# Normalizing the sparse attention's queries in row form, ahead of their split

## The chip, the cores and the metric

The kernel runs on one core of a Trainium2 chip. The metric is the device time of one execution in microseconds (us). TensorE is called PE (its weight loads PEld), VectorE DVE, ScalarE ACT, GpSimd POOL, and the queue that issues most loads SP.

## The reference

A decoder block over 512 tokens of width 2048: RMSNorm, one projection, eight heads of sparse attention (NSA) and four of gated linear attention, an output projection, cross attention over 256 memory tokens, and a SwiGLU. What matters here is how an NSA head treats its queries (cut):

```python
def rms_norm(u, g):
    y = u * lax.rsqrt(jnp.mean(u * u, axis=-1, keepdims=True) + EPS)
    return y * g
qn = rms_norm(q, g_q) * (NSA_DK ** -0.5)          # per head, 128 wide
s = einsum(qn, kc) - slope * (t - cmp_mid);  p = softmax(where(vis, s, NEG))
...
s = einsum(qn, kw) - slope * (t - pos);      p = softmax(...)
```

Each head has three branches: compressed blocks (31 keys, held as 32 columns), selected blocks (512 tokens are 8 blocks of 64, and up to 16 are chosen, so all are taken) and a causal window. The 8 heads share 2 sets of keys and values.

## The kernel before

Every large product runs as three fp32r products of high and low parts (`mm3`: hi·hi, hi·lo, lo·hi, so 2 + 1 matmuls of 128x512 per tile). `split` makes the parts: a copy to fp32r on ACT (hi) and a subtraction on DVE (lo). Weights come by SP into a buffer `w` (2 of them), and are split into `wh` and `wl` (3 each).

The projection of the block's input is walked tile by tile. `in_tile(16 + n)` is one tile of 128 columns: 48 matmuls into a bank `mm`, with 8 calls of `flows.tick()` in it. The heads are Python generators (`nsa_head`, `head_norm`), run in the ticks: `yield n` lets n ticks pass. So a head's steps are written out between the matmuls of the projection of later tiles, and what the generators emit in a tick sets the order on each engine; a scheduler with priorities moves it a little. A tick has 6 matmuls of 128x512 behind it. PSUM has 3 banks `mm`, 2 `s`, 2 `t` and one `o`.

The life of a head: its projected tile (features on partitions, tokens in columns) is split into `Q` hi and lo; the squares (`n`) are summed over the partitions for each token; after W_SUM ticks the sums are used, after W_NORM more the head waits until the head before it has taken its scores (`("s", h - 1)`), and then takes one score block per 2 ticks in a bank `s` (first branch on `KS`, 416 and 512 wide with the 32 compressed columns ahead, second on `KV`), with a bias made by ACT from the distances, a reduction on DVE to the minimum (the scores are negated), and an Exp on ACT. When its head before has left `o`, the P matrices are transposed (PE, into `t`), split into `PH` and `PL` and multiplied with the values into `o`. The end is a normalization of `o` (squares `on`, `column_sums` with `ones_r`).

The head before does not normalize its queries. It keeps them raw but for the gain, and carries one factor per token through the softmax: `sc` (inverse root mean square times the token's own `rc`), `neg = -sc` and `sl = slope / sc`, each of shape 128 x 4 (tile `qs`). To have them with tokens on partitions, it sums the squares by four fp32 matmuls, each with 128 tokens of `n` as weights and the vector `one` (a column of `vecs`) as the moving side, into a bank `s`.

The first head starts ahead of the value weights' stage (`natural(w_vsw, ...)`, with the compression weights `w_c`); heads 1 to 7 are interleaved with the swish gates of the other attention in the order `IN_ORDER`; then the last two gates (`w_r67`) are projected together in two banks, with a tick per 6 matmuls, and `flows.drain()` runs what is left of the heads. The output projection `w_out` follows; its first two tiles (16 products each over the mixed heads, `X`) are filled in between the last heads' steps, and the 16th product needs head 7.

Of the kernel before, what the change touches and what calls it, by code (L numbers as in the profile page):

```python
# [39 lines left out]
IN_ORDER = (1, 2, 8, 3, 9, 4, 10, 5, 11, 6, 12, 7, 13)  # L40
TOFF = (0, 512, 896, 1152)

W_SUM, W_NORM, W_LEVEL = 3, 2, 2

LAG = 3

# [14 lines left out]
def hybrid_block(ctx: ExitStack, tc: tile.TileContext, x_t, mem_t, sv, cmat, umask, w_a, w_r67, w_v, w_vg, w_v3,  # L61
# [17 lines left out]
    def small(tag, bufs):  # L79
        return sb([128, 32], tag, bufs)  # L80
# [7 lines left out]
    def bank(tag):  # L88
        return psp.tile([128, 512], F32, name=tag, tag=tag, bufs={"mm": 3, "s": 2, "t": 2, "o": 1}[tag])
# [3 lines left out]
    def row(tag, dt=F32):  # L93
        return sb([128, 512], tag, BUFS[tag], dt)
# [61 lines left out]
    def split(hi, lo, src, gain=None):  # L156

        if gain is None:
            return S.copy(hi, src), V.tensor_sub(lo, src, hi)  # L159
        return (S.activation(hi, src, AF.Copy, scale=gain),  # L160
                V.scalar_tensor_tensor(lo, src, gain, hi, op0=OP.mult, op1=OP.subtract))
# [85 lines left out]
    def column_sums(sq, cols=T, tag="n", ps="s", wait=1, ahead=0):  # L247

        hi, lo = row(tag, F32R)[:, :cols], row(tag, F32R)[:, :cols]
        with tc.high_priority(offset=ahead):  # L250
            split(hi, lo, sq)
        yield wait
        ps = bank(ps)[:, :cols]
        mm(ps, ones_r, hi, start=True, stop=False)
        mm(ps, ones_r, lo, start=False, stop=True)
        return ps
# [14 lines left out]
        inv_rms(rc, ps[:, :tiles], n, const.tile([128, 32], F32, name="rt", tag="rt", bufs=1)[:, :tiles])  # L271
        return rc

    def head_norm(ps, rs, gain, dst, cols=T):
        q1 = row("q1")[:, :cols]
        if len(rs.shape) == 3:
            V.tensor_mul(q1.rearrange("p (a n) -> p a n", a=2), ps.rearrange("p (a n) -> p a n", a=2), rs)
        else:
            V.tensor_mul(q1, ps, rs)
        sq = row("n")[:, :cols]  # L280
        S.activation(sq, q1, AF.Square)
        pn = yield from column_sums(sq, cols, wait=W_SUM)
        r, t = row("n")[:, :cols], row("n")[:, :cols]
        inv_rms(r, pn, 128, t)
        if isinstance(dst, tuple):
            V.scalar_tensor_tensor(t, q1, gain, r, op0=OP.mult, op1=OP.mult)
            split(*dst, t)
        else:
            V.scalar_tensor_tensor(dst, q1, gain, r, op0=OP.mult, op1=OP.mult)
# [89 lines left out]
    nc.sync.dma_start(cm, cmat[:, 128:768])  # L379
    flows.until(lambda: "col" in norm)  # L380
    rs, rc = norm["row"], norm["col"]
    rc2 = small("rc2", 1)[:, :NT]
    V.tensor_mul(rc2, rc, rc)
    vl = [natural_end(acc, 0, 512, rc, lambda i: row("KV"))]
    um = [row("M").bitcast(U32) for _ in range(2)]
    gkr, gk2, ga = row("st")[:96], row("M", F32R)[:96], row("M", F32R)[:96]
# [330 lines left out]
    def nsa_head(h, ps):  # L717
        kv = h // 4
        slope = 2.0 ** -(h + 1)
        qn = row("Q", F32R), row("Q", F32R)  # L720
        split(*qn, ps, g_q)
        sq = row("n")
        S.activation(sq, ps, AF.Square)
        yield W_SUM
        pn = bank("s")
        for i in range(NT):
            mm(pn[:, i:i + 1], sq[:, 128 * i:128 * i + 128], one, start=True, stop=True)
        qs = triple("qs")
        sc, sl, neg = qs[:, 0], qs[:, 1], qs[:, 2]
        V.tensor_mul(neg, pn[:, :NT], rc2)  # L730
        inv_rms(sc, neg, 128, sl)
        V.tensor_mul(sc, sc, rc)
        V.reciprocal(sl, sc)
        V.tensor_scalar(sl, sl, slope, None, op0=OP.mult)
        V.tensor_scalar(neg, sc, -1.0, None, op0=OP.mult)
        yield W_NORM
        while not {"kc", ("k", 0, kv), ("k", 1, kv)} <= done or h and ("s", h - 1) not in done:
            yield 1
        sm = triple("sm")
        mn = triple("mn")  # L740
        cf = triple("cf")

        def coefficients(b):
            V.reciprocal(cf[:, b, :], sm[:, b, :])
            V.tensor_mul(cf[:, b, :], cf[:, b, :], gates[:, :, 3 * h + b])

        pc, pc3 = sb([128, NT, 32], "pc", 1), sb([128, NT, 3, 32], "pc3", 1)

        def visible(i, s):
            V.scalar_tensor_tensor(pc[:, i], cdist[:, 32 * i:32 * i + 32], sl[:, i:i + 1], s, op0=OP.mult, op1=OP.add)  # L750

        def weigh_blocks():
            V.tensor_reduce(mn[:, 0, :], pc, axis=AX.X, op=OP.min)
            V.tensor_sub(pc, mn[:, 0, :][:, :, None].to_broadcast([128, NT, 32]), pc)
            V.tensor_mul(pc, pc, sc[:, :, None].to_broadcast([128, NT, 32]))
            S.activation(pc, pc, AF.Exp)
            V.reduce_sum(sm[:, 0, :], pc, axis=AX.X)
            coefficients(0)
            V.tensor_mul(pc3, pc[:, :, None, :].to_broadcast([128, NT, 3, 32]),
                         cf[:, 0, :][:, :, None, None].to_broadcast([128, NT, 3, 32]))  # L760

        ps_ = []

        def scale(b):
            coefficients(1 + b)
            for i in range(NT):
                n = 128 * (i + 1)
                pi = ps_[b][:, POFF[i]:POFF[i] + n]
                V.tensor_scalar(pi, pi, cf[:, 1 + b, i:i + 1], None, op0=OP.mult)

        for b in range(2):
            p = sb([128, 1280], "P", 2)
            ps_.append(p)
            for i in range(NT):
                n = 128 * (i + 1)
                pi = p[:, POFF[i]:POFF[i] + n]
                S.activation(pi, dist[:, 512 - n:], AF.Copy, scale=sl[:, i:i + 1])
                s = bank("s")
                q = part(qn, 128 * i, 128)
                c = 32 if b == 0 and i < 3 else 0  # L780
                mm3(s[:, :c + n], q, part(keys[b][kv], 0 if b or c else 32, c + n), start=True, stop=True)
                if c and i == 0:
                    mm3(s[:, 160:192], part(qn, 384, 128), part(keys[0][kv], 0, 32), start=True, stop=True)
                    visible(3, s[:, 160:192])
                if c:
                    visible(i, s[:, :32])
                s = s[:, c:c + n]
                m = mn[:, 1 + b, i:i + 1]
                V.tensor_tensor_reduce(pi, s, pi, scale=1.0, scalar=3e38, op0=OP.add, op1=OP.min, accum_out=m)
                V.tensor_mul(m, m, sc[:, i:i + 1])  # L790
                S.activation(pi, pi, AF.Exp, bias=m, scale=neg[:, i:i + 1], accum_out=sm[:, 1 + b, i:i + 1])
                yield 2 if h < NH - 1 else 1
            if b == 0:
                weigh_blocks()
            scale(b)
        done.add(("s", h))

        while "vc" not in done or h and ("a", h - 1) not in done:
            yield 1
        pct = bank("t")  # L800
        for i in range(NT):
            PE.transpose(pct[:96, 128 * i:128 * i + 128], pc3[:, i].rearrange("p r n -> p (r n)"), ident)
        pcs = row("e", F32R)[:96]
        S.copy(pcs, pct[:96])
        V.tensor_sub(pcs[64:], pct[64:96], pcs[64:])
        o = None
        for b in range(2):
            pt = sb([128, 1280], "PH", PTB, F32R), sb([128, 1280], "PL", PTB, F32R)

            def turn(j):  # L810
                n = 128 * (NT - j)
                tp = bank("t")
                for i in range(j, NT):
                    PE.transpose(tp[:, 128 * (i - j):128 * (i - j) + 128],  # L814
                                 ps_[b][:, POFF[i] + 128 * j:POFF[i] + 128 * j + 128], ident)
                split(*part(pt, TOFF[j], n), tp[:, :n])

            def weigh(j):
                n = 128 * (NT - j)
                mm3(o[:, 128 * j:], part(vsw[j], 256 * b + 128 * kv, 128), part(pt, TOFF[j], n),  # L820
                    start=False, stop=b == 1 and j == NT - 1)

            turn(0)
            yield 2
            if b == 0:
                o = bank("o")
                mm(o, vc[:, 128 * kv:128 * kv + 128], pcs, start=True, stop=False)
            for j in range(1, NT):
                turn(j)
                weigh(j - 1)  # L830
                yield 2
            weigh(NT - 1)
        done.add(("a", h))
        t = row("st" if h < 4 else "M")
        S.copy(t, o)
        sq = row("on")
        S.activation(sq, t, AF.Square)
        pn = yield from column_sums(sq, T, "on", "t", W_SUM)
        r = row("on")
        inv_rms(r, pn, 128, row("on"))  # L840
        V.scalar_tensor_tensor(t, t, vec("g_nsa"), r, op0=OP.mult, op1=OP.mult)
        mix[h] = spill(t) if h < 4 else t
# [963 lines left out]
```

## Time and profile before

| what | value |
|---|---|
| median of 3 runs | 2296.41 us (2295.43 to 2296.8) |
| profiled execution | 2296.01 us, its span 2294.1 us |
| granted clock | 0.999 |
| PE busy | 2282.2 us, 99% of the span |
| PEld, DVE, ACT, POOL busy | 83%, 72%, 52%, 7% |
| chain that ended last | PE 92%, DMA 3%, DVE 3%, ACT 1%, issue 1% |

Reading it: "busy" is the time in which at least one instruction ran on the engine; a busy PE may still issue with gaps between its matmuls. The span is measured on the engines, the time of the execution from outside, 1.9 us more. A line number is that of the code above. In a group "out<-in" stands for the names of the tiles, and "x8" for eight records.

### The profile page before, as it was taken

What the parts mean: (1) busy time and instruction counts of PE and PEld (TensorE: products, weight loads), DVE (VectorE), ACT (ScalarE), POOL (GpSimd) and SP (SyncE); (2) the same over time, 40 slices, a digit from 0 to 9 for tenths busy, and PEclk for the clock granted to TensorE, in tenths of its full rate; (3) what the DMA queues carried; (4) which work ended last, traced back from release to release, by engine and by line L of the source; (5) the groups of instructions that cost most, each with busy time, mean ns of one, the idle gap of its engine ahead of it and who ended that gap; (6) DMA issues with size and microseconds to landing.
All of it is one profiled execution on the core that took longest, in us unless ns stands there. A gap on an engine that the chain in (4) does not pass through costs nothing.

```text
span 2294.1 us, 29540 instructions
## 1 busy us (share of the span) xinstructions
PE 2282.2 (99%) x10773; PEld 1896.1 (83%) x10773; DVE 1663.2 (72%) x2555; ACT 1182.6 (52%) x1855; POOL 163.7 (7%) x240
## 2 busy tenths in 40 slices
PE   9999999999999999999999999999999999999999
PEld 7988888888888888787888888888888888888887
DVE  6478866677775446688788788888887875775685
ACT  6334545566774345665545445554554565444452
POOL 0011100011110000110000000000000000000000
PEclk9999999999999999999999999999999999999999
DMA  6577656466655334685556656565665598766754
GB/s 197 136 192 180 172 157 168 127 173 174 164 170 170 133 134 138 217 233 174 168 182 208 186 162 200 184 191 158 205 201 164 165 326 298 264 233 249 263 209 147
DMA packets 140593, 434.17 MB, mean 189 GB/s; under 512 B 14464, under 2 KB 35200, under 8 KB 136992
## 3 DMA queue, kind: packets, MB, share of 16 engines
q1 hardware_dynamic: 80752, 306.83, 39.8%
q0 software_dynamic: 33824, 96.75, 17.6%
q10 hardware_dynamic: 25872, 28.71, 3.5%
q8 instruction: 84, 1.38, 0.2%
q14 instruction: 61, 0.50, 0.1%
HBM read 390.81 MB, written 94.11 MB: 211 GB/s over the span
## 4 chain that ended last, share of the span: by engine, by line
PE 92%; DMA 3%; DVE 3%; ACT 1%; issue 1%; SPq 0%; DVEq 0%; ACTq 0%
PE mm L99 49%; PE t L99 17%; PE s L99 14%; PE o L99 9%; DVE wl L159 1%; PE t L814 1%; PE s L1377 1%; DMA w<-w_c 1%; DMA raw<-w_down 0%; DMA st<-x_t 0%; DMA w<-w_vsw 0%; ACT wh L159 0%; DMA raw<-w_gu 0%; PE t L1599 0%; DMA w<-w_v 0%
## 5 line engine op out<-in xcount | busy, mean ns | idle before, releaser
L159 ACT CAST qh<-raw 128x1024 fp32r<-128x1024 f32 (+1 forms) x526 | 510.4, 980 | 491.9 <-PE t L99 126.5
L159 DVE TENSOR_TENSOR ql<-raw,qh 128x1024 fp32r<-128x1024 f32 (+1 forms) x526 | 591.4, 1133 | 150.0 <-PE mm L99 52.7
L99 PE MATMUL mm<-X,wh 128*128 128x512 f32 x1600 | 504.5, 395 | 0.0
L99 PEld LDWEIGHTS mm<-X,wh 128*128 128x128 f32 x1600 | 294.3, 188 | 56.2 <-issue 0.8
L99 PE MATMUL t<-qh,PB 128*128 128x512 f32 x968 | 335.9, 392 | 0.0
L99 PE MATMUL mm<-X,wl 128*128 128x512 f32 x800 | 314.0, 393 | 0.1
L99 PE MATMUL mm<-qh,PB 128*128 128x512 f32 x868 | 311.1, 391 | 2.3 <-ACT qh L159 2.0
L159 DVE TENSOR_TENSOR wl<-w,wh 128x1024 fp32r<-128x1024 f32 (+2 forms) x150 | 179.6, 1200 | 157.3 <-ACT wh L159 155.5
L159 ACT CAST wh<-w 128x1024 fp32r<-128x1024 f32 (+2 forms) x150 | 154.2, 1029 | 242.0 <-PE mm L99 171.7
L99 PE MATMUL s<-qh,PB 128*128 128x512 f32 x672 | 232.7, 391 | 0.0
L99 PE MATMUL mm<-qh,PA 128*128 128x512 f32 x640 | 221.8, 390 | 0.0
L99 PEld LDWEIGHTS t<-qh,PB 128*128 128x128 f32 x968 | 182.0, 188 | 37.1
L99 PEld LDWEIGHTS mm<-qh,PB 128*128 128x128 f32 x868 | 163.2, 188 | 37.8 <-ACT qh L159 3.7
L99 PE MATMUL t<-ql,PB 128*128 128x512 f32 x484 | 188.6, 390 | 0.0
L99 PE MATMUL o<-qh,PB 128*128 128x512 f32 x484 | 188.0, 390 | 0.0
L99 PEld LDWEIGHTS mm<-X,wl 128*128 128x128 f32 x800 | 150.3, 188 | 32.4 <-DVE wl L159 1.5
L99 PE MATMUL mm<-ql,PB 128*128 128x512 f32 x434 | 169.9, 391 | 0.1
L99 PEld LDWEIGHTS s<-qh,PB 128*128 128x128 f32 x672 | 126.2, 188 | 25.7 <-ACT qh L159 0.2
L99 PEld LDWEIGHTS mm<-qh,PA 128*128 128x128 f32 x640 | 120.2, 188 | 25.1
L99 PE MATMUL s<-ql,PB 128*128 128x512 f32 x336 | 131.5, 391 | 0.1
L99 PE MATMUL mm<-ql,PA 128*128 128x512 f32 x320 | 124.7, 390 | 0.0
L1279 DVE TENSOR_TENSOR raw<-raw 128x1024 f32<-128x1024 f32 x80 | 97.8, 1223 | 31.4 <-DMA raw<-w_gu 31.4
(501 smaller groups left out, 3452.5 us busy)
## 6 DMA issues: line engine op xcount, KB each, us to landing
raw<-w_gu SPq DMA_DIRECT2D x88, 768.0 KB, 4.4
raw<-w_gu SPq DMA_DIRECT2D x88, 512.0 KB, 3.6
raw<-w_down SPq DMA_DIRECT2D x84, 512.0 KB, 4.7
td<-w_down POOLq DMA_DIRECT2D x66, 512.0 KB, 6.5
w<-w_a SPq DMA_DIRECT2D x60, 512.0 KB, 4.2
raw<-td SPq DMA_DIRECT2D x22, 1024.0 KB, 4.8
PB<-h POOLq DMA_DIRECT2D x35, 512.0 KB, 5.4
h<-T ACTq DMA_DIRECT2D x66, 256.0 KB, 3.9
```

What stands on the lines that cost most here:

```text
L99: last_mm[0] = PE.matmul(*args, **kw)
L159: return S.copy(hi, src), V.tensor_sub(lo, src, hi)
L814: PE.transpose(tp[:, 128 * (i - j):128 * (i - j) + 128], ps_[b][:, POFF[i] + 128 * j:POFF[i] + 128 * j + 128], ident)
L1279: V.tensor_sub(raw[:, 0:1024], raw[:, 0:1024], raw[:, 512:1536])
L1377: PE.transpose(ps[f][:, 128 * i:128 * i + 128], hs[i][:, c:c + 128], ident)
```

## The change

The projected queries go through `head_norm`, as the keys do: times `rs` (the tokens' factor in row form) into `q1`, squares, sums over the partitions by `column_sums` (a split of the squares, two fp32r matmuls of 128x512 with `ones_r`), an inverse root on full rows 128x512, one multiplication by gain and root, and only then the split into `Q`. The factors `sc`, `neg`, `sl` and the products with them are gone; bias and Exp have constants as scale. The bank for the sums is `s` for head 0, `mm` for the others. The wait W_NORM behind the normalization goes from 2 ticks to 7.

```diff
-W_SUM, W_NORM, W_LEVEL = 3, 2, 2
+W_SUM, W_NORM, W_LEVEL = 3, 7, 2
...
-    def head_norm(ps, rs, gain, dst, cols=T):
+    def head_norm(ps, rs, gain, dst, cols=T, sums="s"):
...
-        pn = yield from column_sums(sq, cols, wait=W_SUM)
+        pn = yield from column_sums(sq, cols, ps=sums, wait=W_SUM)
...
-    rc2 = small("rc2", 1)[:, :NT]
-    V.tensor_mul(rc2, rc, rc)
...
         qn = row("Q", F32R), row("Q", F32R)
-        split(*qn, ps, g_q)
-        sq = row("n")
-        S.activation(sq, ps, AF.Square)
-        yield W_SUM
-        pn = bank("s")
-        for i in range(NT):
-            mm(pn[:, i:i + 1], sq[:, 128 * i:128 * i + 128], one, start=True, stop=True)
-        qs = triple("qs")
-        sc, sl, neg = qs[:, 0], qs[:, 1], qs[:, 2]
-        V.tensor_mul(neg, pn[:, :NT], rc2)
-        inv_rms(sc, neg, 128, sl)
-        V.tensor_mul(sc, sc, rc)
-        V.reciprocal(sl, sc)
-        V.tensor_scalar(sl, sl, slope, None, op0=OP.mult)
-        V.tensor_scalar(neg, sc, -1.0, None, op0=OP.mult)
+        yield from head_norm(ps, rs, g_q, qn, sums="mm" if h else "s")
         yield W_NORM
...
-            V.scalar_tensor_tensor(pc[:, i], cdist[:, 32 * i:32 * i + 32], sl[:, i:i + 1], s, op0=OP.mult, op1=OP.add)
+            V.scalar_tensor_tensor(pc[:, i], cdist[:, 32 * i:32 * i + 32], slope, s, op0=OP.mult, op1=OP.add)
...
-            V.tensor_mul(pc, pc, sc[:, :, None].to_broadcast([128, NT, 32]))
...
-                S.activation(pi, dist[:, 512 - n:], AF.Copy, scale=sl[:, i:i + 1])
+                S.activation(pi, dist[:, 512 - n:], AF.Copy, scale=slope)
...
-                V.tensor_mul(m, m, sc[:, i:i + 1])
-                S.activation(pi, pi, AF.Exp, bias=m, scale=neg[:, i:i + 1], accum_out=sm[:, 1 + b, i:i + 1])
+                S.activation(pi, pi, AF.Exp, bias=m, scale=-1.0, accum_out=sm[:, 1 + b, i:i + 1])
```

Line numbers of the changed kernel are 2 lower up to the head, and 18 lower behind it (the reduction L789 is L772, the Exp L791 is L773, the bias L777 is L760, the scaling L769 is L752, the swish lines L857 to L862 are L839 to L844).

In the places below X is an input or a mixed head in two parts, wh and wl are weights. First PE in a head in the middle of the stretch, before: `n` are the squares, `vecs` holds the vector of ones.

```order
L99 MATMUL mm<-X,wh 128x512 x2
L99 MATMUL mm<-X,wl 128x512
L99 MATMUL s<-KS,Q 128x416 x3
L99 MATMUL s<-KS,Q 128x512 x3
L99 MATMUL mm<-X,wh 128x512 x2
L99 MATMUL s<-vecs,n 128x1 x4
L99 MATMUL mm<-X,wl 128x512
L99 MATMUL mm<-X,wh 128x512 x2
L99 MATMUL mm<-X,wl 128x512
L99 MATMUL mm<-X,wh 128x512 x2
```

The same head's sums now:

```order
L99 MATMUL s<-KS,Q 128x160 x3
L99 MATMUL s<-KS,Q 128x32 x3
L99 MATMUL mm<-X,wh 128x512 x2
L99 MATMUL mm<-X,wl 128x512
L99 MATMUL mm<-X,wh 128x512 x2
L99 MATMUL mm<-X,wl 128x512
L99 MATMUL mm<-n,ones_r 128x512 x2
L99 MATMUL mm<-X,wh 128x512 x2
L99 MATMUL mm<-X,wl 128x512
L99 MATMUL mm<-X,wh 128x512 x2
L99 MATMUL mm<-X,wl 128x512
```

Four fp32 matmuls of one column gave way to two of 512 columns in a bank `mm`, and the score blocks of the head before stand elsewhere between the projection's matmuls.

Second, PE at the end of the heads, before: `mm<-X,wh` up to the transposes of P are the last gates' projection, `s<-KS,Q` and `s<-KV,Q` the scores of head 7.

```order
L99 MATMUL mm<-X,wh 128x512 x2
L99 MATMUL mm<-X,wl 128x512
L99 MATMUL s<-KS,Q 128x416 x3
L99 MATMUL s<-KS,Q 128x512 x3
L99 MATMUL mm<-X,wh 128x512 x2
L99 MATMUL s<-KV,Q 128x128 x3
L99 MATMUL mm<-X,wl 128x512
L99 MATMUL mm<-X,wh 128x512 x2
L99 MATMUL s<-KV,Q 128x256 x3
L99 MATMUL mm<-X,wl 128x512
L99 MATMUL mm<-X,wh 128x512 x2
L99 MATMUL mm<-X,wl 128x512
L814 MATMUL t<-ident,P 128x128 x4
```

And now, where the rows of `mm` behind the transposes belong to the output projection:

```order
L99 MATMUL mm<-X,wh 128x512 x2
L99 MATMUL mm<-X,wl 128x512
L99 MATMUL mm<-X,wh 128x512
L99 MATMUL o<-PH,KV 128x128
L99 MATMUL mm<-X,wh 128x512
L99 MATMUL s<-KS,Q 128x416 x3
L99 MATMUL s<-KS,Q 128x512 x3
L99 MATMUL o<-PL,KV 128x128
L99 MATMUL s<-KV,Q 128x128 x3
L99 MATMUL s<-KV,Q 128x256 x3
L99 MATMUL o<-PH,KV 128x128
L796 MATMUL t<-ident,P 128x128 x3
```

Head 7's scores stood among the matmuls of the gates' projection; now they stand behind its last one, with products of head 6's P around them.

Third, ACT at the same place, before (`L858` to `L860` is the swish, `L777` the bias, `L791` the Exp):

```order
L159 CAST PH<-t 128x384
L159 CAST X<-KS 128x512
L159 CAST wh<-w 128x1024
L858 ACTIVATE st<-q_6306 128x512
L777 ACTIVATE P<-cm,qs 128x128
L777 ACTIVATE P<-cm,qs 128x256
L777 ACTIVATE P<-cm,qs 128x384
L777 ACTIVATE P<-cm,qs 128x512
L859 ACTIVATE st<-st,vecs 128x512
L791 ACTIVATE P,sm<-P,mn,qs 128x128
L791 ACTIVATE P,sm<-P,mn,qs 128x256
L860 ACTIVATE st<-st 128x512
```

And now (swish L840 to L842, bias L760, Exp L773):

```order
L773 ACTIVATE P,sm<-P,mn 128x256
L841 ACTIVATE st<-st,vecs 128x512
L773 ACTIVATE P,sm<-P,mn 128x384
L842 ACTIVATE st<-st 128x512
L773 ACTIVATE P,sm<-P,mn 128x512
L739 ACTIVATE pc<-pc 128x128
L840 ACTIVATE st<-q_6216 128x512
L159 CAST PH<-t 128x512
L841 ACTIVATE st<-st,vecs 128x512
L159 CAST PH<-t 128x384
L842 ACTIVATE st<-st 128x512
L159 CAST X<-M 128x512
```

Between head 7's bias and the cast of the next operand of the output projection (`X<-M`) stand now the four Exps of a branch, both gates' swish and two casts of head 6's P; before, several casts of X stood ahead of the bias.

Fourth, DVE in the stage of the value weights, before, around head 0's normalization:

```order
L161 SCALAR_TENSOR_TENSOR Q<-mm,vecs,Q 128x512
L159 TENSOR_TENSOR Q<-e,Q 128x4x64 x2
L613 TENSOR_TENSOR e<-KV,vecs 128x8x31 x2
L730 TENSOR_TENSOR qs<-s,rc_539 128x4
L243 SCALAR_TENSOR_TENSOR qs<-qs 128x4
L244 TENSOR_SCALAR qs<-qs 128x4
L245 TENSOR_TENSOR qs<-qs 128x4
L732 TENSOR_TENSOR qs<-qs,rc 128x4
L733 RECIPROCAL qs<-qs 128x4
L735 TENSOR_SCALAR qs<-qs 128x4
L734 TENSOR_SCALAR qs<-qs 128x4
L159 TENSOR_TENSOR wl<-w,wh 128x1024
```

And now:

```order
L159 TENSOR_TENSOR wl<-w,wh 128x1024
L279 TENSOR_TENSOR q_3197<-mm,rs 128x512
L159 TENSOR_TENSOR wl<-w,wh 128x1024
L159 TENSOR_TENSOR n<-n 128x512
L243 SCALAR_TENSOR_TENSOR n<-s,n 128x512
L244 TENSOR_SCALAR n<-n 128x512
L159 TENSOR_TENSOR wl<-w,wh 128x1024
L245 TENSOR_TENSOR n<-n 128x512
L286 SCALAR_TENSOR_TENSOR n<-q_3197,vecs,n 128x512
L159 TENSOR_TENSOR Q<-n,Q 128x512
L159 TENSOR_TENSOR wl<-w,wh 128x1024 x2
L734 SCALAR_TENSOR_TENSOR pc<-cm,s 128x32 x2
```

The split of Q (L161) and eight small operations on 128x4 gave way to seven operations on 128x512, spread between the splits of weights, and head 0's first block (`pc<-cm,s`) comes two splits of weights further behind.

## The prediction

> **What bounds the kernel now.** I read the page's first and fourth parts, then the stretch of the heads by windows, then the waits and the order of time in two windows. The lines of the engines and of the chain:
>
> ```profile
> PE 2282.2 (99%) x10773; PEld 1896.1 (83%) x10773; DVE 1663.2 (72%) x2555; ACT 1182.6 (52%) x1855; POOL 163.7 (7%) x240
> PE 92%; DMA 3%; DVE 3%; ACT 1%; issue 1%; SPq 0%; DVEq 0%; ACTq 0%
> ```
>
> PE is the bound, and the chain lies on it. So only matmuls taken away and stalls of PE count. The stretch with the heads falls in three windows (columns: stretch, its length, busy us and instructions of PE, PEld, DVE, ACT, POOL, then the granted clock, DMA share and rate):
>
> ```profile
> 345.00:405.00 60.00, 58.66 (x297) 48.72 (x296) 37.21 (x88) 32.76 (x59) 4.45 (x6) 1.00 0.62 168
> 405.00:640.00 235.00, 235.00 (x1237) 198.06 (x1238) 167.30 (x489) 150.40 (x330) 36.31 (x49) 1.00 0.59 156
> 640.00:692.00 52.00, 51.89 (x256) 41.21 (x255) 41.89 (x98) 37.60 (x78) 5.89 (x11) 1.00 0.61 197
> ```
>
> In the middle, heads 1 to 7 beside the projection, PE is never idle, and DVE and ACT are free for 29% and 36% of it. In the first window, the value weights, PE idles 1.3 us; in the last, the end of the heads, 0.1. The clock is full in all three.
>
> **The sums on PE.** One group of sums before, and two fp32r matmuls with `ones_r` in the end of a head, as the change uses them (start, length, what):
>
> ```profile
> 423.56 0.95 PE L99 MATMUL s<-vecs,n 128*128 128x1 f32 x8
> 424.38 0.71 PE L99 MATMUL mm<-X,wh 128*128 128x512 f32 x2
> 424.93 0.39 PE L99 MATMUL mm<-X,wl 128*128 128x512 f32 x1
> ...
> 499.98 0.61 PE L99 MATMUL t<-on,ones_r 128*128 128x512 f32 x2
> 500.43 0.62 PE L99 MATMUL mm<-X,wh 128*128 128x512 f32 x2
> ```
>
> From the start of the sums to the `wl` matmul at 424.93 are 1.37 us. Two matmuls of 512 columns are 0.45 (499.98 to 500.43), so the pair at 424.38 accounts for 0.45 of this and the sums for 0.92. The new sums take 0.45. That is 0.47 less per head, 3.8 us for eight, straight on the path. It can't be much more (nothing of the group is left); it is nothing if the gaps were filled by something else, which I see nowhere.
>
> Here a rule speaks against the change. The Trainium skill, "TensorE: Matmul & The Clock Gate" (Step-by-step: what each phase is for), says "throughput is purely `N cycles`": one column a cycle; "FP8 and Floating Point Precision" (TensorE Precision Notes) gives true fp32 four passes. By that four fp32 matmuls of one column are 16 cycles, next to nothing, and two of 512 are 1024: the change would add 0.45 us per head instead of saving 0.47. The rows say otherwise for the old group, 0.92 us; for the new one rule and row agree.
>
> **DVE and ACT, per head.** Rows of the middle window (mean ns is the last number before the bar):
>
> ```profile
> L790 DVE TENSOR_TENSOR mn<-mn,qs 128x1 f32<-128x1 f32 x48 | 7.5, 157 | 1.1
> L161 DVE SCALAR_TENSOR_TENSOR Q<-mm,vecs,Q 128x512 fp32r<-128x512 f32 x7 | 5.2, 747 | 0.0
> L857 DVE TENSOR_TENSOR q<-mm,rs 128x512 f32<-128x512 f32 x6 | 4.1, 692 | 7.0 <-PE mm L99 7.0
> L243 DVE SCALAR_TENSOR_TENSOR on<-t,on 128x512 f32<-128x512 f32 x5 | 3.5, 691 | 0.4
> L841 DVE SCALAR_TENSOR_TENSOR st<-st,vecs,on 128x512 f32<-128x512 f32 x4 | 3.0, 752 | 0.1
> L244 DVE TENSOR_SCALAR on<-on 128x512 f32<-128x512 f32 x5 | 2.1, 426 | 0.1
> L755 DVE TENSOR_TENSOR pc<-pc,qs 128x128 f32<-128x128 f32 x6 | 1.7, 290 | 0.0
> L730 DVE TENSOR_TENSOR qs<-s,rc 128x4 f32<-128x4 f32 x7 | 1.1, 162 | 5.8 <-PE s L99 5.7
> ...
> L160 ACT ACTIVATE Q<-mm,vecs 128x512 fp32r<-128x512 f32 x7 | 4.8, 681 | 0.0
> L240 ACT ACTIVATE on<-t,vecs 128x512 f32<-128x512 f32 x6 | 4.1, 683 | 0.0
> L242 ACT ACTIVATE on<-on 128x512 f32<-128x512 f32 x6 | 3.8, 640 | 0.0
> L241 ACT ACTIVATE on<-on 128x512 f32<-128x512 f32 x6 | 3.8, 626 | 0.0
> L159 ACT CAST on<-on 128x512 fp32r<-128x512 f32 x6 | 3.7, 610 | 0.0
> L240 ACT ACTIVATE qs<-qs,vecs 128x4 f32<-128x4 f32 x7 | 2.0, 286 | 4.8 <-DVE qs L730 4.8
> ```
>
> DVE loses the split's low part (0.75), eight small operations (0.16 each by L730, 1.3), one of 128x128 (0.29) and eight of 128x1 (1.26): 3.6 us. It gains the product with `rs` (0.69 as L857), two low parts and the last product of the root (0.69 each, as L243), L243, L244 (0.43) and the gain (0.75 as L841): 4.6. ACT loses the gain (0.68) and three small ones (0.29 or less each, 0.8) and gains three of 128x512 (0.68, 0.63, 0.64) and two casts (0.61 each): 1.7 more. In the middle, with 34 us per head (7 groups of sums, L730, in 235 us) and DVE and ACT with 10 and 12 free of it, both are hidden behind PE; if the cover went, it would cost 1.0 and 1.7 us a head. The factors `rc2`, once, are as small as L730. No DMA of this kernel is added or taken away; the orders to POOL that hang on ticks move with them.
>
> **The banks.** Sums in `mm` need one of three banks, for the 3 ticks at most that one DVE and one ACT read take; the projection's result leaves its bank with the first product. PE is never late here before, so I take nothing; a missed bank would be a stall of under 1 us (one product, 0.69) per head.
>
> **The first stage, 345 to 405.** PE waits here for the splits of the weights, and the splits stand in DVE's queue with head 0's softmax:
>
> ```profile
> 389.30 0.74 PE L99 MATMUL mm<-wh,X 128*128 128x512 f32 x2 [0.79 <-ACT wh L159]
> 390.56 0.50 PE L99 MATMUL mm<-wl,X 128*128 128x512 f32 x1 [0.28 <-DVE wl L159]
> ...
> 378.63 0.69 DVE L789 CUSTOM_DVE_ANT_0 P<-s,P 128x512 f32<-128x512 f32 x1
> 381.12 1.28 DVE L769 TENSOR_SCALAR P<-P,cf 128x128 f32<-128x128 f32 x4
> 382.31 2.35 DVE L159 TENSOR_TENSOR wl<-w,wh 128x1024 fp32r<-128x1024 f32 x2
> 389.28 1.23 DVE L159 TENSOR_TENSOR wl<-w,wh 128x1024 fp32r<-128x1024 f32 x1 [4.62 <-ACT wh L159]
> ```
>
> From 378.63 to 382.31 DVE does the last reduction, splits and the four scalings, and only then the two low parts whose buffers the next load of weights waits for. In the changed order head 0's blocks come two splits of weights later, so this knot comes loose: the 0.79 and 0.28 us and more may go (PE idles 1.3 us here by the window; a stall also slows the matmul behind it, so I bound what is to be had at twice that, 2.5, an estimate). But five operations of full rows are now ahead (2.0 us more of DVE than the small ones), and the knot may come again two splits later, with 1.5 us of cost at most if it hits as hard as here with those 2.0 on top. I take -0.4, nearer to the loss because the softmax isn't gone but moved.
>
> **The end of the heads.** The wait of 7 ticks for 2 moves every head's scores 5 ticks back, some 7 us (a tick is 6 matmuls, 1.36). For heads 0 to 6 there is projection beside them. Head 7's scores came while the last gates' projection still ran; now they come after it. What ran there before:
>
> ```profile
> 655.50:664.70 9.20, 9.20 (x43) 7.55 (x42) 8.48 (x25) 9.19 (x22) 1.11 (x3) 1.00 0.76 235
> ...
> L99 PE MATMUL mm<-X,wh 128*128 128x512 f32 x23 | 7.3, 395 | 0.0
> L99 PE MATMUL mm<-X,wl 128*128 128x512 f32 x11 | 4.3, 392 | 0.0
> ...
> L791 ACT ACTIVATE P<-P,mn,qs 128x128 f32<-128x128 f32 (+3 forms) x4 | 2.6, 644 | 0.0
> L777 ACT ACTIVATE P<-cm,qs 128x128 f32<-128x128 f32 (+3 forms) x4 | 1.9, 547 | 0.0
> L859 ACT ACTIVATE st<-st,vecs 128x512 f32<-128x512 f32 x2 | 1.4, 711 | 0.0
> L860 ACT ACTIVATE st<-st 128x512 f32<-128x512 f32 x2 | 1.2, 622 | 0.0
> L858 ACT ACTIVATE st<-q 128x512 f32<-128x512 f32 x2 | 1.2, 620 | 0.0
> L791 ACT ACTIVATION_READ_ACCUMULATOR P<-P,mn,qs 128x1 f32 x4 | 0.7, 186 | 0.0
> ```
>
> In these 9.2 us ACT was busy for 9.19: four Exps (2.6 and 0.7 for reading their sums), four biases (1.9), two swishes (3.8). PE didn't mind: it had 34 matmuls of `mm`. In the changed order that projection is over when head 7's first scores come, and PE has the output projection only as far as ACT and DVE have split its operands. From head 6's last transposes to the first matmul on the next operand PE has 18 matmuls of `mm`, twelve of scores, and a few of `o` and `t`: some 7.2 us at 0.225 per 512 columns. ACT has ahead of the cast of that operand the Exps, the swishes, 0.3 of a small Exp, and three casts of about 0.55: 9.1. Short by 1.9. From there to the third operand PE has some 5.9 us, and ACT another set of biases and Exps (5.2), and casts: 8.0. Short by 2.1. Of the 4.0 I take 3.5, for ACT may be ahead at the start; before, PE idled 0.1 here. Ends: 1 us if ACT is ahead by all of a bias set, and 6 if DVE, 8.48 busy of 9.20 in the same stretch, adds its own lateness. Behind the 16th operand the program is the same.
>
> **The sum.** The profiled execution took 2296.0 (span 2294.1, 1.9 around it), 0.4 below the median of the runs shown. 2296.0 - 3.8 - 0.4 + 3.5 = 2295.3. What can be told from no change is 0.2%, 4.6 us: 2291.8 to 2301.0 by the median. With the ends together the likeliest case lies between 2296.0 - 3.8 - 2.5 + 1 = 2290.7 and 2296.0 - 3.8 + 1.5 + 6 = 2299.7.
>
> **The rivals.**
> The tail stays covered and the first stage comes loose: PE's saving stands alone. For it speaks that head 6's transposes and the output projection can be taken in another order than I walked, and that all these shortages are small beside a queue on ACT which I counted by hand; against it, ACT's 9.19 of 9.20. 2296.0 - 3.8 - 2.5 + 0 = 2289.7, faster. Chance 0.20.
> The end runs dry: all of ACT's work that ran under the gates' projection (9.2 us) lies bare, as PE waits on every operand. 2296.0 - 3.8 - 0.4 + 9.2 = 2301.0, and with the first stage's loss 2302.9: slower. It decides from a tail of 8.8 us on. Against it: 18 matmuls of filler are ready at its start. Chance 0.12.
> The change doesn't do what it says on PE: the old group's 0.92 us is a place where PE waited for `n` or the bank and would wait again. 2296.0 - 0.4 + 3.5 = 2299.1. The rows show no wait marked on it, so 0.04, within the bound.
> The old sums cost next to nothing and the new ones their columns: +0.45 per head, 2296.0 + 3.6 - 0.4 + 3.5 = 2302.7. Chance 0.02; the Trainium skill's rule above is this one.
>
> **The numbers.** The likeliest, 0.62, gives 2295.3. Faster holds the first rival and a little of the likeliest's lower end: 0.22. Slower holds the second's upper part and the last: 0.13. The rest, 0.65, is the same. The range from 2289.7 to 2299.7 takes in the first rival and leaves out the bare end.
>
> **What would show it.** In the profile after: two records `mm<-n,ones_r` with 0.45 us to the next start, no `s<-vecs,n` in the heads; PE's instructions fewer, its busy time about 3.8 lower but for gaps; the middle window with PE idle for nothing. In the first stage, the waits on `wh` and `wl` smaller or some splits later. At the end, idle time of PE in front of `mm<-X,wh` put down to ACT or DVE `X`, 3 to 4 us, with ACT full. I am wrong if PE waits in the middle for `Q` or a bank, or if no wait at all stands at the end.

## The result, and the profile after

The changed kernel takes 2309.03 us (median of 6 runs, 2306.24 to 2311.63) against 2296.72 for the kernel before: ratio 1.0052, interval 1.0042 to 1.0062. It is slower by 12 us, outside the range that was forecast. The profiled execution took 2311.63, the slowest of the six; its span was 2309.8.

The page's engines and chain, after:

```profile
PE 2294.0 (99%) x10725; PEld 1893.7 (82%) x10725; DVE 1670.7 (72%) x2466; ACT 1183.0 (51%) x1863; POOL 164.4 (7%) x240
PE 91%; DMA 3%; DVE 3%; issue 1%; ACT 1%; SPq 0%; DVEq 0%; ACTq 0%
```

PE has 48 matmul records less (the sums' eight records a head became two) and yet is busy for 11.8 us more. That is the first sign: not PE waiting, but PE's matmuls taking longer. The three stretches of the prediction, after (length, PE busy and count, PEld, DVE, ACT, POOL, granted clock, DMA share and rate):

```profile
345.00:405.00 60.00, 57.56 (x272) 47.33 (x271) 32.80 (x67) 25.29 (x43) 5.06 (x6) 0.97 0.60 163
405.00:640.00 235.00, 234.95 (x1192) 195.42 (x1191) 173.61 (x409) 151.50 (x328) 37.42 (x50) 1.00 0.61 160
640.00:692.00 52.00, 50.64 (x260) 40.39 (x260) 42.10 (x102) 39.08 (x89) 5.36 (x10) 1.00 0.44 135
```

In the middle PE is as full as before, with 1192 matmuls for 1237 in the same 235 us. The sums of seven heads make 42 of the 45 (56 records became 14), but those are 3.3 us that should have let other matmuls in. A count in a stretch with changed work proves little, so I looked where the two programs are the same instruction for instruction, first at their start, then in the output projection (PE's busy time and count, granted clock, DMA). Before:

```profile
20.00:60.00 40.00, 39.44 (x201) 1.00 0.53 161
...
700.00:880.00 180.00, 180.00 (x804) 1.00 0.44 147
```

And after:

```profile
20.00:60.00 40.00, 39.76 (x197) 1.00 0.50 152
...
700.00:880.00 180.00, 180.00 (x780) 1.00 0.41 139
```

PE is never idle from 700 to 880 in either, the granted clock is 1.00 in both, no operand is late, and it issues 804 matmuls before and 780 after: 3% less. Start to start, the 512-column matmuls there come every 226.7 ns before, and alternate between some 229 and 237.5 ns after (from the records' starts, in twelve microseconds without an exception). No edit touches this code. A transfer much later, the first of `PA` by POOL, lies at 928.47 before and here after:

```profile
941.09 0.54 POOL L1180 DMA_DIRECT2D PA<-x  x1
```

So 12.6 us are lost by then. Behind it the matmuls come every 226.7 ns in both, and the spans part by 3 us more. That part of the program is the same in all the kernels here, and from this transfer to the end it took between 1365.4 and 1368.8 us in their traces, the kernel before at the low end and the changed one at the high end; I take these 3 us for what differs from execution to execution.

The sums on PE, after, are as forecast: two matmuls, 0.47 us to the next start.

```profile
429.77 0.63 PE L99 MATMUL mm<-n,ones_r 128*128 128x512 f32 x2
430.24 0.63 PE L99 MATMUL mm<-X,wh 128*128 128x512 f32 x2
```

What PE waited for in the first stage (340 to 420) and then at the end of the heads (640 to 710), and the granted clock behind the first:

```profile
PE mm L99 <- DVE wl L159: 1.9, 2, 1.6
PE mm L99 <- ACT wh L159: 0.5, 1, 0.5
...
PE mm L99 <- ACT X L159: 0.8, 1, 0.8
PE o L99 <- DVE PL L159: 0.3, 1, 0.3
```

```profile
378.00:383.00 5.00, 3.37 (x9) 0.72 0.42 116
```

The end dries out where the prediction said (`mm` waiting for `X`, ACT late). The stall in the first stage is larger than before, and behind it the clock was granted at 0.72 for a while: eight matmuls came every 0.43 us. These waits, and the 1.4 us that the clock took (an estimate: 0.28 of 5 us), are a few microseconds, and do not explain 12.

### The profile page after: what moved, and what is told of

The parts are those of the page before. It is cut to its first block, busy times and chain, and to the rows that moved or that the text cites. A ratio compares the mean times of both kernels' runs of the same rounds, so it can differ in the third digit from the quotient of the medians.

```text
span 2309.8 us, 29351 instructions
## 1 busy us (share of the span) xinstructions
PE 2294.0 (99%) x10725; PEld 1893.7 (82%) x10725; DVE 1670.7 (72%) x2466; ACT 1183.0 (51%) x1863; POOL 164.4 (7%) x240
## 4 chain that ended last, share of the span: by engine, by line
PE 91%; DMA 3%; DVE 3%; issue 1%; ACT 1%; SPq 0%; DVEq 0%; ACTq 0%
PE mm L99 50%; PE t L99 16%; PE s L99 14%; PE o L99 9%; DMA raw<-w_gu 1%; DVE ql L159 1%; PE t L796 1%; DMA st<-x_t 1%; PE s L1359 1%; DMA w<-w_vsw 1%; DMA raw<-w_down 1%; DVE wl L159 0%; DMA w<-w_c 0%; PE t L1581 0%; DMA w<-w_v 0%
## 5 line engine op out<-in xcount | busy, mean ns | idle before, releaser
L99 PE MATMUL mm<-X,wh 128*128 128x512 f32 x1600 | 511.0, 398 | 0.8 <-ACT X L159 0.8
```

The source lines that it names most:

```text
L99: last_mm[0] = PE.matmul(*args, **kw)
```

## The experiments

What differs in untouched code is the place of the buffers. Buffers come from two pools per partition: the lower holds X, P, PH, PL, Q, n and others, from the bottom up; the upper holds wh, wl, w, ones_r, KV, M and others, and is laid against the top of the memory. The change drops two small tiles of the upper pool, `rc2` (128 bytes) and `qs` (2 x 128). The pool is 384 bytes shorter, and so all that lies below `rc2` starts 384 bytes higher: `wh` at 134400 for 134016, `KV` (between the two tiles) 256 higher; X stays at 28288. All of the following have the instructions of the kernel that they start from, in the same order, unless an edit says otherwise. "Distance" is the difference of the two start addresses, less its whole multiples of 256 bytes. "Matmuls" is PE's count in the window 700 to 880, all at a granted clock of 1.00; the ratio is to the kernel before, on the same chip.

| run | distance of X and wh, modulo 256 | matmuls | median us | ratio (95%) |
|---|---|---|---|---|
| before | 0 | 804 | 2296.3 to 2297.0 | 1 |
| changed | 128 | 780 | 2309.03 | 1.0052 (1.0042, 1.0062) |
| pad384 | 0 | 805 | 2298.66 | 1.0008 (0.9998, 1.0017) |
| pad128 | 0 | 805 | 2298.99 | 1.0009 (0.9999, 1.0018) |
| pad256 | 128 | 786 | 2309.22 | 1.0055 (1.0038, 1.0072) |
| old_pad128 | 128 | 786 | 2306.90 | 1.0040 (1.0026, 1.0055) |
| old_pad64 | 64 | 797 | 2302.14 | 1.0024 (1.0013, 1.0035) |
| old_moving128 | 128 | 787 | 2307.66 | 1.0043 (1.0029, 1.0057) |
| old_both128 | 0 | 804 | 2297.26 | 1.0001 (0.9992, 1.0010) |
| wait2 | 0 | 805 | 2295.61 | 0.9999 (0.9990, 1.0008) |
| wait2_head0 | 0 | 805 | 2296.47 | 1.0000 (0.9991, 1.0008) |
| wait4 | 0 | 804 | 2295.00 | 0.9988 (0.9979, 0.9997) |
| old_wait7 | 0 | 805 | 2308.69 | 1.0053 (1.0041, 1.0066) |

**The place of the buffers.** Four kernels with nothing but unused space added. pad384 has the dropped tiles back where they were:

```diff
     rs, rc = norm["row"], norm["col"]
+    small("rc2", 1)
...
         qn = row("Q", F32R), row("Q", F32R)
+        triple("qs")
```

> The changed kernel, instruction for instruction, with the two small tiles that the change dropped (rc2, qs; 384 bytes of a partition) kept as unused space at their old places, so that every buffer lies where it lay before the change. Theory A (the place of the buffers): the changed kernel's matmuls of 512 columns issue every 232 to 233 ns up to 950 us where those of before issue every 227, also in code that the change doesn't touch, since wh and wl lie 384 bytes further; with the old places the interval goes back to 227 and the time falls by about 11 us, to 2298 (2296 to 2300). Rival B (the order of the work: late scores, first stage, tail): 2309, as the changed kernel. Rival C (the place counts, but by something else than a step of 256 bytes): as A here.

pad128 and pad256 have one or two tiles of 128 bytes near the top of the upper pool instead, and old_pad128 is the kernel before with one:

```diff
+        small("gap", 1)          # pad256: small("gap", 2)
         pc, pc3 = sb([128, NT, 32], "pc", 1), sb([128, NT, 3, 32], "pc3", 1)
```

> The changed kernel with one unused tile of 128 bytes of a partition, ahead of pc, so that wh, wl, ones_r, KV and M lie 128 bytes lower. Theory A: the distance of weights and moving operand counts modulo 256 bytes (0 is full rate, 128 is slow); here X, Q, P, n and wh, wl, KV, M all agree modulo 256, so the interval is 227 ns up to 950 us and the time is 2296 (2293 to 2299), no worse than with 384 bytes. Rival B: 2309. Rival C (any other period, or the plain distance from the old place): a third of the way, 2305, or no change, 2309.

> The changed kernel with two unused tiles of 128 bytes, so that wh, wl, KV and M lie 256 bytes lower. Theory A: modulo 256 nothing has changed, so it stays at 2309 (2306 to 2311) with intervals of 232 ns. Rival B: 2309 too. Rival C: two thirds of the way back, 2301, or as with 384 bytes, 2298.

> The kernel before, instruction for instruction, with one unused tile of 128 bytes ahead of pc, so that wh, wl, ones_r, KV and M lie 128 bytes lower. Theory A: the weights now lie 128 bytes off modulo 256, as in the changed kernel: intervals of 232 ns up to 950 us and 2307 (2304 to 2311), with nothing of the change in it. Rival B: 2296.6, no change. Rival C: a third of the loss, 2300, or none.

The window 700 to 880 in pad384, pad128, pad256 and old_pad128:

```profile
700.00:880.00 180.00, 180.00 (x805) 1.00 0.44 148
```

```profile
700.00:880.00 180.00, 180.00 (x805) 1.00 0.44 148
```

```profile
700.00:880.00 180.00, 180.00 (x786) 1.00 0.42 140
```

```profile
700.00:880.00 180.00, 180.00 (x786) 1.00 0.41 139
```

All four came out as theory A had it, three of them within 1 us of its number and pad128 at the edge of its range. 128 and 384 bytes cure, 256 does nothing, and the kernel before becomes slow with 128 bytes of nothing. Order and instructions (B) are refuted as the main cause: with the old places the same instructions take 10.4 us less (2309.03 to 2298.66). The slow kernels differ a little among themselves (780 matmuls in the changed kernel, 786 and 787 in the others); why stays open.

The Trainium skill, "TensorE: Matmul & The Clock Gate" (Step-by-step: what each phase is for), says that PE reads weights and the moving operand by two independent ports, so that loading the next weights takes no bandwidth from the running matmul. These runs differ: the rate hangs on how the two operands lie to each other. By what path they disturb each other no run shows.

Is it the distance, or the weights' own address? old_moving128 shifts X and its pool instead; old_both128 shifts both:

```diff
     pool_b = held.enter_context(tc.tile_pool(name="sbb", bufs=1))
+    pool_b.tile([128, 32], F32, name="gap0", tag="gap0", bufs=1)
```

> The kernel before with an unused tile of 128 bytes at the start of the lower pool: X, n, Q, P, PH, PL lie 128 bytes higher, the weights wh, wl and KV, M where they were. Theory A (the distance of the two operands of a matmul modulo 256): slow, 2307, intervals of 231 to 233 ns up to 950 us. Rival E (the weights' own address counts, 128 modulo 256 is good): no change, 2296.3 and 227 ns.

> The kernel before with both unused tiles: X and its pool 128 bytes higher, and wh, wl, KV, M 128 bytes lower, so that X and the weights are again 0 apart modulo 256. Theory A: the two shifts cancel, 2296.3 (2294 to 2299) and 227 ns. Rival E: slow as with the weights' shift alone, 2307.

```profile
700.00:880.00 180.00, 180.00 (x787) 1.00 0.42 139
```

```profile
700.00:880.00 180.00, 180.00 (x804) 1.00 0.44 148
```

Either shift alone costs 10 to 11 us, and the two cancel. It is the distance (E refuted). How far must it be off? old_pad64 is the kernel before with a tile of 64 bytes:

> The kernel before with an unused tile of 64 bytes, so that wh, wl, KV and M lie 64 bytes lower: their distance to X is 64 bytes modulo 128 and modulo 256. Theory A says only that 0 modulo 256 is full rate and 128 is slow. If the rule is a step of 256 bytes with any other distance slow, 2307 and intervals of 232 ns; if the clash is at 128 alone, 2296.8 and 227; if it grows with the distance, between the two, 2302.

```profile
700.00:880.00 180.00, 180.00 (x797) 1.00 0.43 146
```

2302.14, half of the loss. Here X is the moving side, and the interval is 229 ns, a third of the way from 226.7 to 232.7; at 20 to 60 us, where X is the weights and wh moves, it is 233, as slow as at 128. So 64 bytes off costs a third one way round and all of it the other way, which none of the three cases held. That the time is the 2302 of the third case is luck: it is an average of the two directions, not a cost that grows with the distance. Why stays open; no run looked inside.

**The wait of 7 ticks.** With the places back, pad384 shows what the rest of the change does. PE in the first stage:

```profile
374.26 0.49 PE L99 MATMUL mm<-wh,X 128*128 128x512 f32 x1 [0.90 <-ACT wh L159]
376.39 0.50 PE L99 MATMUL mm<-wl,X 128*128 128x512 f32 x1 [1.63 <-DVE wl L159]
```

and DVE just ahead of them:

```profile
373.31 0.18 DVE L730 RECIPROCAL cf<-sm 128x4 f32<-128x4 f32 x1 [0.88 <-ACT P L775]
373.52 0.17 DVE L731 TENSOR_TENSOR cf<-cf,gates 128x4 f32<-128x4 f32 x1
373.72 1.28 DVE L754 TENSOR_SCALAR P<-P,cf 128x128 f32<-128x128 f32 x4
374.91 0.28 DVE L774 CUSTOM_DVE_ANT_0 P<-s,P 128x128 f32<-128x128 f32 x1
375.12 1.22 DVE L159 TENSOR_TENSOR wl<-w,wh 128x1024 fp32r<-128x1024 f32 x1
```

The knot of softmax and weights is back, some splits from where it was: the low part of the weights stands in DVE's queue behind the scalings of head 0's first branch, and DVE itself had waited 0.88 us for an Exp. PE waits 2.5 us here. At the end of the heads:

```profile
657.32 0.73 PE L99 MATMUL mm<-X,wh 128*128 128x512 f32 x2 [0.84 <-ACT X L159]
658.32 0.50 PE L99 MATMUL o<-PL,KV 128*128 128x512 f32 x1 [0.27 <-DVE PL L159]
```

Two marks bound the stretch of the heads: the first matmul on `fold`, at the end of the first stage, and the first transfer of `PA`. Before:

```profile
404.89 0.65 PE L99 MATMUL t<-q,fold 128*64 128x256 f32 x2 [0.23 <-ACT q L638]
928.47 0.54 POOL L1198 DMA_DIRECT2D PA<-x  x1
```

And in pad384:

```profile
405.90 0.65 PE L99 MATMUL t<-q,fold 128*64 128x256 f32 x2 [0.49 <-ACT q L637]
928.59 0.54 POOL L1182 DMA_DIRECT2D PA<-x  x1
```

From the one to the other are 523.6 us before and 522.7 in pad384, 0.9 less.

Four kernels set the wait apart, three from pad384 and one from the kernel before:

```diff
-W_SUM, W_NORM, W_LEVEL = 3, 7, 2
+W_SUM, W_NORM, W_LEVEL = 3, 2, 2          # wait2; wait4: 3, 4, 2
...
-        yield W_NORM
+        yield W_NORM if h else 2            # wait2_head0
...
-W_SUM, W_NORM, W_LEVEL = 3, 2, 2
+W_SUM, W_NORM, W_LEVEL = 3, 7, 2          # old_wait7
```

> The changed kernel with its buffers at their old places (as pad384) and W_NORM back at 2 ticks, so that the scores come as early as before. Theory A (the three terms of the prediction stand, measured in the trace of pad384 as -3.8 us for the sums, about +1.8 for a new stall in the first stage and +2.4 for the end of the heads, and only the buffers' place was missed): the last two go, 2298.7 - 1.8 - 2.4 = 2294.5 (2293 to 2296), PE stalls of 1.7 us or less in the last stretch. Rival D (7 ticks are needed: with 2, the longer normalization comes too late and PE waits for Q in every head): over 2300, with waits of PE on Q in the middle stretch.

> As pad384 (old places, W_NORM 7), but head 0 alone waits 2 ticks: its softmax comes early in the first stage, and the other heads and the end stay as in the changed kernel. Theory A: the first stage's new stall of 3 us at 373 goes or moves, the end still costs 2.4 us: 2298.7 - 1.8 = 2296.9 (2295 to 2298.5). If the stall comes from the normalization's own rows on DVE and not from the wait, it stays: 2298.7.

> The kernel before with W_NORM 7 for 2 and nothing else; the buffers keep their places. Theory A: no gain from the sums, and the end dries as in the changed kernel (+2.4), the first stage changes by 0 to +1.8: 2296.8 + 2.4 to 4.2 = 2299.2 to 2301. If the end's cost came from the normalization in row form and not from the wait, 2296.8.

wait2 came at 2295.61, in A's range. Of D's waits in the middle there is one of 0.2 us, on `Q`: 7 ticks weren't needed. But its profiled execution kept a stall in the first stage, where PE waited 1.8 us for a `wh` whose cast had waited for its load, and the clock fell behind it (387 to 395):

```profile
387.00:395.00 8.00, 5.86 (x22) 4.36 (x21) 2.45 (x2) 2.44 (x3) 0.00 (x0) 0.79 0.51 173
```

So the first stage ended 1.7 us later than before in this execution, not earlier. wait2_head0, 2296.47 with 2296.9 expected, has in the first stage waits of 0.7 and 0.3 us, close to the kernel before, and at the end 0.8 and 0.3, as with 7 ticks. The stall at 374 hangs on head 0's wait, then, and not on the rows of the normalization.

old_wait7 is a miss: 2308.69, where 2299.2 to 2301 was expected. The interval of its matmuls is 226.7 ns, so it isn't the place of the buffers. The stall in the first stage is there with the old normalization too (waits of 1.8 and 0.8 us). PE's three longest waits from 640 to 710, and two stretches there:

```profile
PE o L99 <- DVE PL L159: 1.5, 1, 1.5
PE mm L99 <- ACT X L159: 0.9, 1, 0.9
PE o L99 <- ACT PH L159: 0.8, 1, 0.8
```

```profile
656.00:664.00 8.00, 4.83 (x20) 3.34 (x21) 6.75 (x22) 5.79 (x14) 1.45 (x3) 0.89 0.36 114
664.00:670.00 6.00, 6.00 (x24) 5.15 (x24) 3.16 (x10) 3.87 (x10) 1.08 (x2) 0.57 0.36 114
```

PE was busy for 4.83 of 8 us, and then for 6 us "busy" at a granted clock of 0.57. The wait of 7 ticks alone brings a drought at the end, and here it lasts longer than in pad384 (3.2 us in these three waits, for 1.1) and takes the clock down with it. The longest wait, on `PL`, stands behind the four products of both swishes in DVE's queue, where pad384 has one such product just ahead of its `PL`:

```profile
660.37 1.28 DVE L861 TENSOR_TENSOR q<-q,st 128x512 f32<-128x512 f32 x2
661.58 1.28 DVE L862 TENSOR_TENSOR st<-st,q 128x512 f32<-128x512 f32 x2
662.78 1.15 DVE L159 TENSOR_TENSOR PL<-t,PH 128x512 fp32r<-128x512 f32 x2
```

`PA` came at 937.27, 8.8 us later than before, in this execution; some 3.5 of these are the clock (an estimate: 0.11 of 8 us and 0.43 of 6). By the medians 7 ticks cost 12.4 us on the old form (2308.69 against 2296.28) and some 3 on the new one (2298.66 against 2295.61; these two ran on different chips, and their intervals against the kernel before overlap). The old softmax has more work on both queues, a DVE product behind each reduction and ACT instructions with a factor per token; that this is what makes the late scores so dear there is not shown, for the order on DVE differs too.

wait4 looks for a middle:

> As pad384 (changed kernel, buffers at their old places) with W_NORM 4, between 2 (2295.6) and 7 (2298.7): head 7's scores come about 3 us later than with 2. Theory A: the stalls at the end grow with what of head 7 comes behind the last gates' projection, so the end costs about 1 of the 2.4 us, and the first stage something between: 2296.5 (2294.5 to 2298). If the end has a step (all or nothing), it is as 2 ticks, 2295.6, or as 7, 2298.7.

PE's waits in it, in the first stage and at the end:

```profile
PE t L99 <- ACT q L637: 0.4, 1, 0.4
PE mm L99 <- DVE wl L159: 0.3, 1, 0.3
...
PE o L99 <- ACT on L821: 0.4, 1, 0.4
PE s L99 <- DVE mn L774: 0.2, 1, 0.2
```

2295.00, at least as quick as wait2 (their intervals overlap) and the one version here that is faster than the kernel before, by 0.1% with an interval of 0.03 to 0.21%, which is thin for one of twelve kernels compared. Both stretches are nearly free of waits. The time lies in A's range and, within the noise, fits the step as well (2295.6, as with 2 ticks); the two are not parted.

Yet the missing waits didn't shorten the stretch. The two marks in wait4:

```profile
404.39 0.65 PE L99 MATMUL t<-q,fold 128*64 128x256 f32 x2 [0.40 <-ACT q L637]
927.14 0.54 POOL L1182 DMA_DIRECT2D PA<-x  x1
```

From `fold` to `PA` are 522.7 us here, as in pad384, and 523.6 in wait2, as before the change. So of the 3.3 us that seven heads' sums give back, 0.9 at most came out at the end of the stretch with any of the waits. In pad384 1.1 of the missing 2.4 stand as waits at the end of the heads; where the rest goes, and what is missing in wait4 and wait2, is not shown. wait2's time lies in A's range, then, but the two terms that A lets go are not seen to go in its trace.

## Why the prediction was wrong

- The step that failed is a cost put at nothing without a reason: the prediction took all instructions outside the places named for the same as before ("Behind the 16th operand the program is the same"), and so gave them the same durations. It costed the removal of `rc2` as one small instruction ("The factors `rc2`, once, are as small as L730") and that of `qs` by the small operations on it, and never the place of what lies beside them. Their removal moved the weights against their moving operands by 128 bytes modulo 256. That made the 512-column matmuls of X with wh or wl 1 to 3% longer on the mean (229.1 ns in pad384 and 232.6 in the changed kernel from 420 to 640, 226.8 and 233.2 from 700 to 880) until the pools are given up, near 950 us: 10.4 us of the 12.3, by pad384. None of the rivals held it.
- The sums on PE: right. 0.92 us became 0.47, with 0.45 forecast. That the 3.8 us come out whole in the time is not borne out: the stretch with seven of the heads became 0.9 us shorter with the places held, not 3.3.
- DVE and ACT hidden in the middle, the banks free: right. PE waited for nothing between 405 and 640 in the changed kernel.
- The first stage: mis-sized, and with the wrong sign. -0.4 was taken; by pad384 the stage ends 1.0 us later (`t<-q,fold` at 405.90 for 404.89), with head 0's own gain of 0.5 in it, and pad384's execution was 0.3 ahead of that of before at 320 us, so about +1.8. "The knot may come again two splits later" was the sentence that held.
- The end of the heads: the mechanism was right, the size too high. 3.5 was taken, with 3 to 4 us of idle time as its sign. PE waited there 0.8 us for `X`, on ACT, and 0.3 for `PL`, on DVE, in pad384 and on the slow places alike. The 2.4 us that are missing from the 3.3 of the sums are more than that, and wait4 misses as much without these waits, so 2.4 is what the stretch lost and 1.1 what is shown of the end.
- The sum of these three is -3.8 + 1.8 + 2.4 = +0.4, less the 0.3 that pad384 was ahead: `PA` lies at 928.59, 0.1 behind before. (The 1.8 and the 2.4 are read off these same marks, so the sum is no test of them.) With the places held the kernel is within 0.2% of before, as the likeliest case had it, if not by its number: 2298.66 for 2295.3, the range ending at 2299.7. That it comes so near is partly luck, for the first stage was taken 2.2 too low and the end too high.
- The rule on columns, weighed as a rival (+0.45 a head): refuted by the same rows of PE, as argued.

## What to carry to other kernels

Where a kernel becomes slower with no wait in it, compare the number of matmuls in a window that the change does not touch: if it differs at the same clock, look at where the buffers lie, for a dropped tile of 128 bytes can move a whole pool. For matmuls like these (128x512 fp32r) lay stationary and moving operands at the same address modulo 256 bytes, and fix the layout before judging a change of this size. A later start for a step at the end of a stage can run past the filler work that hid it, and a stall there can cost nearly double when the clock falls behind it (in wait2 2.1 us of waits, and by an estimate 0.21 of 8 us, 1.7, of clock).

## What the runs showed of the hardware

- The rate of 128x512 fp32r matmuls at full clock: 226.7 ns with both operands 0 apart modulo 256 bytes, 232 to 233 on the mean at 128, and at 64 either 229 or 233, by which of the two is the weights (20 to 60 and 700 to 880 us). At 0 and 128 it holds whichever buffer is shifted, and with X as weights as well as with X as the moving side. In the same trace the pair of wh and M, 128 apart before, went from 231 to 234 ns to 228 to 230 when the change brought it to 0, while X went the other way; these are few matmuls and scatter.
- The granted clock fell to 0.57 to 0.79 for some microseconds behind stalls of PE of 2 to 4 us (378, 387 and 664 in three kernels), but not behind one of 2.5 us in pad384. pad128, which has pad384's instructions in pad384's order, stalled for 2.8 us at the same place, and there the clock fell (0.86 over 370 to 395, for 1.00 in pad384). Which stall does it is not settled here.
- ACT instructions with a constant as scale are shorter than those with a factor per token. The Exps and the biases over the whole run, before:

```profile
L791 ACT ACTIVATE P<-P,mn,qs 128x128 f32<-128x128 f32 (+1 forms) x64 | 41.5, 649 | 11.3 <-DVE mn L790 10.6
L777 ACT ACTIVATE P<-cm,qs 128x128 f32<-128x128 f32 (+1 forms) x64 | 31.9, 553 | 19.0 <-PE t L814 19.0
```

And after:

```profile
L773 ACT ACTIVATE P<-P,mn 128x128 f32<-128x128 f32 (+1 forms) x64 | 35.5, 555 | 13.8 <-DVE mn L772 13.8
L760 ACT ACTIVATE P<-cm 128x128 f32<-128x128 f32 (+1 forms) x64 | 26.3, 462 | 0.0
```

That is 0.09 us on each, 1.4 us a head, which the prediction's sum for ACT left out. The Trainium skill, "ScalarE: Activation LUTs" (What ACT_TABLE_LOAD costs), gives 93 ns for each operand of this kind, and the rows agree.
